# A hybrid attention/RG-LRU step: sums of layer 0 kept in place, first-token products for four blocks, held recurrences, and another grouping of the last columns

## The chip, the cores and the metric

The kernel runs on one core of one Trainium2 chip. The core has five engines, each with a queue of its own that it works off in order: PE (TensorE: matmuls and transposes; its weight loads are shown as PEld), DVE (VectorE), ACT (ScalarE), POOL (GpSimd, which here clears small tiles and issues DMAs) and SP (SyncE, which here only issues DMAs). Matmuls write to PSUM accumulators; DVE and ACT read them out. The metric is the device time of one execution in microseconds (us), as the median of the runs of one kernel.

## The reference, cut to what matters

```python
def reference(x_prompt, x_sample, c, cache_k, cache_v, state_lru, c_ctx, ...):
    y_p, y_s = x_prompt, x_sample            # 128 context tokens, 512 latent tokens, width 2048
    for l in range(2):
        sh, sc, ga = adaln(cond, w_mod[l], b_mod[l])     # once for context, once for latents
        h = rms_norm(y, g_pre[l]) * (1.0 + sc) + sh
        if l == 0: m = attention mixer(h)    # ends in (o * silu(g)) @ w_out_attn
        else:      m = lru_mixer(h)          # below
        y = y + ga * rms_norm(m, g_post[l])

def lru_mixer(h, h0_fwd, h0_bwd, w_in, conv_w, conv_b, w_a, b_a, w_x, b_x, lam, w_out):
    xb, gb = jnp.split(h @ w_in, 2, axis=-1)
    xb = centred_depthwise_conv(xb, conv_w, conv_b)          # width 4
    for d in (forward, backward):
        a, b = rglru_coeffs(xb, w_a[d], b_a[d], w_x[d], b_x[d], lam[d])
        hs[d] = linear_scan(a, b, h0[d], reverse=d)          # h[t] = a[t] * h[t-1] + b[t]
    return ((hs[0] + hs[1]) * silu(gb)) @ w_out, final states

def rglru_coeffs(x, w_a, b_a, w_x, b_x, lam):                # 8 diagonal blocks of 256 columns
    r = sigmoid(block_diag(x, w_a) + b_a); i = sigmoid(block_diag(x, w_x) + b_x)
    a = exp(8 * r * log_sigmoid(lam))
    return a, sqrt(1 - a * a) * i * x
```

## The kernel before, in words

All tokens are handled together: five tiles of 128 tokens, m = 0 to 3 the latents, m = 4 the context (in the transposed form 644 columns, with small gaps). Each fp32 operand is split into a high and a low part ("hi" and "lo" for activations, "wh" and "wl" for weights), and each product is three matmuls. Weights come from memory in pieces of 1 MB into the four buffers of the tile "raw" (load_w, on SP's queue). split_w turns half a piece into wh (ACT, L179) and wl (DVE, L180), of which there are three pairs.

The order of instructions on each engine is set by the framework's planner when the kernel is built: it walks the program in source order as priority, and puts next on an engine what is ready by its own estimate. On the chip each engine keeps that order. A tile of a pool takes one of a fixed number of buffers ("bufs"), and a new tile under the same tag waits until an earlier one has had its last reader.

The second half of the program, in order:

- The output projection of layer 0 (out_proj, gemm_nat) goes over four groups of 512 columns. A group has three accumulators of the tile "pd": tiles (0, 1), (2, 3) and (4). There are four such accumulators of two PSUM banks each (pool "ps2"). Each is read out with the gate into the tile oG (L780) and squared for its norm (L783). The last group is done in two passes, first tiles (0, 1), then (2, 3) and (4) (LAST, L41).
- finish0 (L803), for each tile: load x into a buffer of "raw" (SP), sum x + r * oG into that buffer (DVE, L797), store it as x1_s (POOL, L808), square and sum (ACT, L810), normalise from that buffer into oG (DVE, L812). Then transpose oG (PE, L825), scale and shift, and write hi and lo of those tokens. It is a generator, so that its steps stand between pieces of other products.
- While tiles 2, 3 and 4 go through finish0, PE multiplies the first 256 tokens (tiles 0, 1) with columns of w_in_lru (gemm_T_cols, matmuls of 256 columns): for blocks 0 and 1, both the x half and the gate half. The results wait in two of the four accumulators (p0s).
- Then eight blocks of 256 columns. Blocks 0 and 1 multiply the other 388 columns, x half and gate half; blocks 2 to 7 multiply all tokens (gemm_T, two matmuls of 322 columns each). The x half is copied to "xp" (one buffer), convolved on DVE (conv, L869 to L876, into xc, xh and xl), the gate half becomes gb (ACT tanh, DVE). Then for each half f of the block: four groups of 12 matmuls, each into an accumulator "pd" read out by an ACT sigmoid (L937) into R or I (two buffers each), then the recurrence: tanh, exp and square root on ACT with table loads between them, products and two scans on DVE, and a store to y_s on POOL (L941 to L961).
- The output projection of layer 1 has the same form; finish1 (L985) loads x1_s into "raw" (L990), sums (L995) and stores the outputs (L996). The final states are transposed and stored by final_state, called by late (L999) when four pieces of weights have been used. gate_cols prepares the gates for it during blocks 3 to 6 and the projection.

## Time and profile before

| | us |
|---|---|
| median of 3 runs (lowest to highest) | 1954.33 (1953.74 to 1959.88) |
| the profiled execution, its own time | 1955.32 |
| its span, first to last instruction | 1953.6 |
| PE busy in the span | 1883.5 (96%) |
| DVE busy | 1323.9 (68%) |
| ACT busy | 865.0 (44%) |
| POOL busy | 133.1 (7%) |
| mean granted TensorE clock | 0.991 of 2.4 GHz |

The profiled execution stands for all runs: its time is within 1 us of their median. A row of a timeline has the start, the duration, the engine and line, the operation, the tiles written and read (out<-in), the size, and in brackets how long the engine had been idle and what ended that. Line numbers are those of the kernel before. Matmuls follow each other in a pipeline, so a matmul's shown duration is longer than the distance to the next one; distances or whole stretches give the rate. "PEclk" is the granted clock as a share of 2.4 GHz, so 0.5 is the level of 1.2 GHz.

### The profile page before, as it was taken

What the parts mean: (1) busy time and instruction counts of PE and PEld (TensorE: products, weight loads), DVE (VectorE), ACT (ScalarE), POOL (GpSimd) and SP (SyncE); (2) the same over time, 40 slices, a digit from 0 to 9 for tenths busy, and PEclk for the clock granted to TensorE, in tenths of its full rate; (3) what the DMA queues carried; (4) which work ended last, traced back from release to release, by engine and by line L of the source; (5) the groups of instructions that cost most, each with busy time, mean ns of one, the idle gap of its engine ahead of it and who ended that gap; (6) DMA issues with size and microseconds to landing.
All of it is one profiled execution on the core that took longest, in us unless ns stands there. A gap on an engine that the chain in (4) does not pass through costs nothing.

```text
span 1953.6 us, 26764 instructions
## 1 busy us (share of the span) xinstructions
PE 1883.5 (96%) x10857; PEld 1673.2 (86%) x10857; DVE 1323.9 (68%) x1846; ACT 865.0 (44%) x1255; POOL 133.1 (7%) x212
## 2 busy tenths in 40 slices
PE   4999999999999899999999989899999999999996
PEld 1567887879999899998888889899999999987885
DVE  3237759758375389998857774875685675798645
ACT  4441223222121388881223565666456456742232
POOL 0000000000000001110000000110010010020000
PEclk9999999999999999999999999999999999999998
DMA  9996535536454212225636673323232232546445
GB/s 342 343 318 209 166 109 183 178 123 200 149 178 158 74 38 74 74 97 174 204 130 211 226 263 109 122 77 117 94 102 92 94 100 64 175 140 212 146 149 216
DMA packets 194892, 304.20 MB, mean 156 GB/s; under 512 B 7232, under 2 KB 124608, under 8 KB 191952
## 3 DMA queue, kind: packets, MB, share of 16 engines
q1 hardware_dynamic: 188800, 276.20, 42.6%
q0 software_dynamic: 5968, 26.28, 3.7%
q8 instruction: 85, 1.39, 0.3%
q14 instruction: 39, 0.32, 0.0%
HBM read 273.03 MB, written 29.43 MB: 155 GB/s over the span
## 4 chain that ended last, share of the span: by engine, by line
PE 83%; DVE 6%; ACT 5%; issue 2%; DMA 2%; SPq 1%; POOL 0%; DVEq 0%; ACTq 0%; POOLq 0%
PE pd L184 22%; PE pd L185 22%; PE pd L186 22%; PE pd L215 2%; PE pm L276 2%; PE pd L217 2%; PE pd L218 2%; PE ph L631 1%; PE pg L184 1%; ACT L937 1%; PE pg L186 1%; PE pg L185 1%; PE sp L184 1%; PE sp L186 1%; PE ph L184 1%
## 5 line engine op out<-in xcount | busy, mean ns | idle before, releaser
L179 ACT CAST wh<-raw 128x1024 fp32r<-128x1024 f32 x248 | 258.1, 1048 | 604.8 <-PE pd L186 323.6
L180 DVE TENSOR_TENSOR wl<-raw,wh 128x1024 fp32r<-128x1024 f32 x248 | 301.4, 1221 | 237.5 <-ACT wh L179 236.6
L184 PE MATMUL pd<-wh,hi 128*128 128x512 f32 x1040 | 410.4, 395 | 5.8 <-ACT pd L783 3.3
L185 PE MATMUL pd<-wl,hi 128*128 128x512 f32 x1040 | 409.9, 394 | 0.0
L186 PE MATMUL pd<-wh,lo 128*128 128x512 f32 x1040 | 409.7, 394 | 0.0
L184 PE MATMUL pd<-hi,wh 128*128 128x322 f32 x1280 | 399.2, 312 | 0.0
L186 PE MATMUL pd<-hi,wl 128*128 128x322 f32 x1280 | 397.0, 310 | 1.1 <-DVE wl L180 1.1
L185 PE MATMUL pd<-lo,wh 128*128 128x322 f32 x1280 | 397.5, 311 | 0.0
L186 PEld LDWEIGHTS pd<-hi,wl 128*128 128x128 f32 x1280 | 241.6, 189 | 1.6 <-DVE wl L180 1.6
L185 PEld LDWEIGHTS pd<-lo,wh 128*128 128x128 f32 x1280 | 242.2, 189 | 0.1
L184 PEld LDWEIGHTS pd<-hi,wh 128*128 128x128 f32 x1280 | 241.4, 189 | 0.5 <-ACT wh L179 0.3
L184 PEld LDWEIGHTS pd<-wh,hi 128*128 128x128 f32 x1040 | 195.5, 188 | 52.5 <-ACT pd L783 3.7
L186 PEld LDWEIGHTS pd<-wh,lo 128*128 128x128 f32 x1040 | 195.4, 188 | 45.9
L185 PEld LDWEIGHTS pd<-wl,hi 128*128 128x128 f32 x1040 | 195.4, 188 | 45.4 <-DVE wl L180 0.3
L741 DVE SCALAR_TENSOR_TENSOR ga<-raw,cT,ga 128x512 f32<-128x512 f32 x256 | 175.5, 744 | 15.2 <-DMA ga<-b_mod 12.4
L395 DVE SCALAR_TENSOR_TENSOR ga<-raw,cT,ga 128x1024 f32<-128x1024 f32 x120 | 149.7, 1278 | 28.1 <-DMA raw<-w_mod 27.5
L215 PE MATMUL pd<-hi,wh 128*128 128x256 f32 (+1 forms) x256 | 80.5, 314 | 6.4 <-ACT wh L179 4.7
L184 PE MATMUL pd<-xh,wh 128*128 128x322 f32 x256 | 81.1, 318 | 5.2 <-ACT xh L875 4.4
L185 PE MATMUL pd<-xl,wh 128*128 128x322 f32 x256 | 80.0, 313 | 0.0
L218 PE MATMUL pd<-hi,wl 128*128 128x256 f32 (+1 forms) x256 | 79.9, 312 | 0.0
L217 PE MATMUL pd<-lo,wh 128*128 128x256 f32 (+1 forms) x256 | 79.8, 312 | 0.0
L186 PE MATMUL pd<-xh,wl 128*128 128x322 f32 x256 | 79.8, 312 | 0.0
(233 smaller groups left out, 2807.3 us busy)
## 6 DMA issues: line engine op xcount, KB each, us to landing
raw<-w_mod SPq DMA_DIRECT2D x64, 1024.0 KB, 5.2
raw<-w_in_lru SPq DMA_DIRECT2D x40, 1024.0 KB, 5.3
raw<-w_in_attn SPq DMA_DIRECT2D x36, 1024.0 KB, 6.1
raw<-w_mod SPq DMA_DIRECT2D x64, 512.0 KB, 8.4
raw<-w_out_attn SPq DMA_DIRECT2D x20, 1024.0 KB, 6.0
raw<-w_out_lru SPq DMA_DIRECT2D x20, 1024.0 KB, 5.3
g_s<-qf POOLq DMA_DIRECT2D x16, 322.0 KB, 3.4
raw<-g_s SPq DMA_DIRECT2D x16, 322.0 KB
```

The source lines that it names most:

```text
L179: S.copy(wh, src)
L180: V.tensor_tensor(wl, src, wh.bitcast(F32), op=sub)
L184: PE.matmul(out, ah, bh, start=first, stop=False)
L185: PE.matmul(out, ah, bl, start=False, stop=False)
L186: PE.matmul(out, al, bh, start=False, stop=last)
L215: PE.matmul(outs[f], wh[:, c], hi[:, k, t], start=(k == 0 and first[f]), stop=False, skip_group_check=True)
L217: PE.matmul(outs[f], wh[:, c], lo[:, k, t], start=False, stop=False, skip_group_check=True)
L218: PE.matmul(outs[f], wl[:, c], hi[:, k, t], start=False, stop=(k == KT - 1), skip_group_check=True)
L276: PE.matmul(pm[32 * j:32 * j + 32], c32[:, kb * 4 + j], raw[:, j * 512:j * 512 + 512], start=(kb == 0), stop=(kb == 3))
L395: V.scalar_tensor_tensor(acc[c], w2[:, k2], cT[:, k, c:c + 1], acc[c], op0=mult, op1=add)
L631: PE.transpose(pt[:, c * 128:c * 128 + 128], P[:, b, c * 128:c * 128 + 128], ident)
L741: V.scalar_tensor_tensor(acc[:, c], raw[:, k4 * 512:k4 * 512 + 512], cT[:, kb * 4 + k4, c:c + 1], acc[:, c], op0=mult, op1=add)
```

## The change

1. finish0: the sum goes into oG itself, and the store and the normalisation work on oG. x of tiles 0, 1 and 3 comes into "raw" as before; x of tiles 2 and 4 comes in two halves of 1024 columns into a buffer of the gates ("Gc") and one of the gate accumulation ("ga"), loaded on POOL's queue: tile 2's at the end of the first pass, tile 4's after tile 2's sum. The square's unused output goes to a tile under the tag "v".
2. The first 256 tokens are multiplied with the x halves of blocks 0 to 3 (NB1 = 4) and no gate halves. Blocks 0 to 3 then multiply 388 columns for x, and all tokens for the gate.
3. The recurrence becomes the function recur. For f = 1 of blocks 0, 1 and 2 it is held and called in the next block, behind that block's convolutions.
4. Layer 1's last column group is done as tiles (0, 1) and (4), then (2) and (3) in accumulators of their own, whose squares go to an SBUF tile. finish1 sums in place in halves; x1 of tiles 0, 1 and 4 comes in halves through two buffers on POOL's queue. final_state is called two pieces later.

```diff
-NB1 = 2
-LAST = [[(0, 1)], [(2, 3), (4,)]]
+NB1 = 4
+LAST = [[[(0, 1)], [(2, 3), (4,)]], [[(0, 1), (4,)], [(2,), (3,)]]]
...
+    def x_halves(p):
+        a = p.tile([128, 2, 512], F32, name="Gc", tag="Gc", bufs=2)
+        b = gpool.tile([128, 2, 512], F32, name="ga", tag="ga")
+        return [t.rearrange("p c n -> p (c n)") for t in (a, b)]
...
-            for grp in ([PAIRS] if n < 3 else LAST):
+            for grp in ([PAIRS] if n < 3 else last):
...
-                        S.activation(a[:, j], a[:, j], AF.Square, accum_out=ss[:, m, n:n + 1])
+                        sq = gpool.tile([128, 512], F32, name="gp", tag="gp") if grp is LAST[1][1] else a[:, j]
+                        S.activation(sq, a[:, j], AF.Square, accum_out=ss[:, m, n:n + 1])
...
+    def halves():
+        return [(t, lambda a, b=b: a[:, b * 1024:b * 1024 + 1024]) for b, t in enumerate(x_halves(pd))]
+    def fetch(m, pieces):
+        held_x[m] = pieces
+        for x, cut in pieces:
+            G.dma_start(x, cut(x_rows(m)))
...
-                xt = x1_tile(m, oG, r, j, x_rows(m))
-                G.dma_start(x1_s[m], xt)
+                pieces = held_x.pop(m) if m in held_x else whole(rawp.tile([128, 2048], F32, name="raw", tag="raw"))
+                if m in (0, 1, 3):
+                    SY.dma_start(pieces[0][0], x_rows(m))
+                for x, cut in pieces:
+                    V.scalar_tensor_tensor(cut(oG[:, m]), cut(oG[:, m]), r[:, j:j + 1], x, op0=mult, op1=add)
+                if m == 2:
+                    fetch(4, halves())
+                G.dma_start(x1_s[m], oG[:, m])
                 sx = small.tile([128, 1], F32, name="sx", tag="sx")
-                S.activation(oG[:, m], xt, AF.Square, accum_out=sx)
+                S.activation(pd.tile([128, D], BF16, name="vj", tag="v", bufs=2), oG[:, m], AF.Square, accum_out=sx)
                 r1 = rstd_of(sx, 1, D, "r1")
-                V.tensor_scalar(oG[:, m], xt, r1, None, op0=mult)
+                V.tensor_scalar(oG[:, m], oG[:, m], r1, None, op0=mult)
...
+        if len(grp) == 1:
+            fetch(2, halves())
...
     for blk in range(NB1):
-        p0 = psd()
-        p0s.append(p0)
-        for e in range(2):
-            gemm_T_cols([p0[:, e, 0:256], p0[:, e, 256:512]], w_l, e * D + blk * 256, slice(0, 256),
-                        lambda: next(rest, None), (True, False))
+        if blk % 2 == 0:
+            p0s.append(psd())
+        p0 = p0s[blk // 2][:, blk % 2]
+        gemm_T_cols([p0[:, 0:256], p0[:, 256:512]], w_l, blk * 256, slice(0, 256),
+                    lambda: next(rest, None), (True, False))
...
+    def recur(blk, f, R, I, xc, gb):
...
         if blk < NB1:
-            p0 = p0s[blk]
-            t2 = slice(256, TW)
+            p0 = p0s[blk // 2][:, blk % 2]
             n2 = TW - 256
-            px, pg = psd(), psd()
...
+            px = psd()
+            gemm_T_cols([px[:, 0, :n2], px[:, 1, :n2]], w_l, blk * 256, slice(256, TW), lambda: None, (True, True))
+            src = [[(1, p0[:, f * 256:f * 256 + 256]), (257, px[:, f, :n2])] for f in range(2)]
         else:
             acc = gemm_T(w_l, blk * 256)
+            src = [[(1 + h * TH, acc[f][:, h, :TH]) for h in range(2)] for f in range(2)]
+        for f in range(2):
+            xp = pad()
+            for at, a in src[f]:
+                S.copy(xp[:, at:at + a.shape[1]], a)
+            xcs.append(conv(xp, blk * 2 + f))
+        while held:
+            recur(*held.pop())
+        acc = gemm_T(w_l, D + blk * 256)
...
+            if f and blk < NB1 - 1:
+                held.append((blk, f, R, I, xcs[f][0], gbs[f]))
+            else:
+                recur(blk, f, R, I, xcs[f][0], gbs[f])
...
     def finish1(grp, oG, ss):
...
+                for h in range(2):
+                    c = slice(h * D // 2, (h + 1) * D // 2)
+                    y = oG[:, m, c]
+                    if m in (2, 3):
+                        x = raw[:, c]
+                    else:
+                        x = pf.tile([128, 1024], F32, name="xr", tag="xr", bufs=2)
+                        G.dma_start(x, x1_s[m][:, c])
+                    V.scalar_tensor_tensor(y, y, r[:, j:j + 1], x, op0=mult, op1=add)
+                    (SY if m in (2, 3) else G).dma_start(dst[:, c], y)
+                yield
...
-        if kb == 4:
+        if kb == 6:
             final_state()
```

## Rows read from the trace of the kernel before

**Rows 1.** The page, part 1: busy time of each engine, its share of the span, and its instructions.

```profile
PE 1883.5 (96%) x10857; PEld 1673.2 (86%) x10857; DVE 1323.9 (68%) x1846; ACT 865.0 (44%) x1255; POOL 133.1 (7%) x212
```

**Rows 2.** Whom PE waited for from 1100 us to the end: the line waited for, us in total, times, the longest.

```profile
PE pd L215 <- ACT wh L179: 4.7, 1, 4.7
PE pd L184 <- ACT xh L875: 4.4, 1, 4.4
PE pd L184 <- ACT pd L783: 3.3, 1, 3.3
PE pd L215 <- ACT I L937: 1.7, 1, 1.7
...
PE pd L184 <- ACT R L937: 0.5, 1, 0.5
```

**Rows 3.** Stretches (us from the span's start) and their length; busy us and instructions of PE, PEld, DVE, ACT and POOL; the granted TensorE clock; the DMA engines' share; GB/s. In order: two stretches around the end of layer 0's projection, the first-token stretch, a piece of it with matmuls of 256 columns alone, a product of 388 columns, blocks 0 and 1, the products of block 2, the gates of block 2.

```profile
1102.00:1120.00 18.00, 18.00 (x111) 15.91 (x110) 14.06 (x23) 11.90 (x22) 0.00 (x0) 1.00 0.50 174
1120.00:1140.00 20.00, 14.70 (x114) 14.29 (x113) 16.89 (x36) 10.39 (x13) 1.60 (x3) 0.89 0.91 321
1114.50:1173.20 58.70, 53.40 (x434) 52.94 (x434) 46.77 (x78) 37.42 (x56) 1.73 (x5) 0.94 0.75 250
1162.00:1173.00 11.00, 11.00 (x95) 11.00 (x95) 8.90 (x15) 8.07 (x15) 0.14 (x2) 1.00 0.59 187
1173.20:1190.30 17.10, 17.10 (x99) 17.10 (x98) 5.80 (x5) 4.30 (x5) 0.00 (x0) 1.00 0.44 132
1173.20:1224.30 51.10, 48.89 (x290) 48.15 (x288) 25.77 (x28) 29.84 (x37) 0.27 (x4) 1.00 0.33 103
1224.30:1278.90 54.60, 50.18 (x289) 49.92 (x290) 39.99 (x40) 36.55 (x43) 8.83 (x16) 0.97 0.33 109
1278.90:1336.10 57.20, 57.20 (x387) 57.06 (x386) 44.84 (x45) 26.76 (x29) 8.48 (x16) 1.00 0.38 122
1336.10:1350.60 14.50, 14.44 (x98) 14.18 (x97) 3.94 (x4) 14.20 (x16) 0.00 (x0) 1.00 0.01 1
```

**Rows 4.** The chain of work that ended last, in order of time: start, us, what.

```profile
1111.94 0.23 PE pd L184
...
1127.62 8.57 DMA raw<-w_in_lru
...
1152.83 1.75 PE pd L825 x16
```

**Rows 5.** Timeline of POOL: the issue of tile 3's store of x1.

```profile
1126.76 0.53 POOL L808 DMA_DIRECT2D x_s<-raw  x1 [2.86 <-DVE raw L797]
```

**Rows 6.** Timeline of DVE: the sum of tile 1, the normalisations of tiles 0 and 1, and of tile 3.

```profile
1086.82 2.35 DVE L797 SCALAR_TENSOR_TENSOR raw<-oG,rr,raw 128x2048 f32<-128x2048 f32 x1
...
1094.28 2.48 DVE L812 TENSOR_SCALAR oG<-raw,rr 128x2048 f32<-128x2048 f32 x2
...
1133.13 1.28 DVE L812 TENSOR_SCALAR oG<-raw,rr 128x2048 f32<-128x2048 f32 x1
```

**Rows 7.** The five stores of x1 (L808), from issue to landing.

```profile
DMA to landing us min/median/max: 4.1/5.3/8.2
```

**Rows 8.** Timeline of DVE: in block 0 the second convolution's first step, its last (xl), the recurrence of f = 0 from its first to its last product; in block 1 the first convolution's first step, the second's last; in block 2 the second gate accumulator's readout.

```profile
1197.67 0.61 DVE L869 TENSOR_SCALAR xc<-xp,VB 128x644 f32<-128x644 f32 x1
...
1203.07 0.83 DVE L876 TENSOR_TENSOR xl<-xc,xh 128x644 fp32r<-128x644 f32 x1 [0.46 <-ACT xh L875]
...
1217.68 1.50 DVE L950 TENSOR_TENSOR I<-I,xc 128x1288 f32<-128x1288 f32 x1 [5.08 <-ACT I L937]
...
1236.62 0.82 DVE L960 SCALAR_TENSOR_TENSOR R<-R,gb 128x642 f32<-128x642 f32 x1
...
1245.98 0.61 DVE L869 TENSOR_SCALAR xc<-xp,VB 128x644 f32<-128x644 f32 x1
...
1264.78 0.83 DVE L876 TENSOR_TENSOR xl<-xc,xh 128x644 fp32r<-128x644 f32 x1
...
1338.41 0.82 DVE L914 SCALAR_TENSOR_TENSOR gb<-gb,pd 128x644 f32<-128x644 f32 x1
```

**Rows 9.** The sixteen stores of a recurrence's result (L961), from issue to landing.

```profile
DMA to landing us min/median/max: 2.5/2.7/3.6
```

**Rows 10.** Timeline of ACT in the gates of block 2: a table load, the first sigmoid, then (left out) a tanh, a load, exp and a load, and the second sigmoid.

```profile
1337.86 1.28 ACT L937 ACT_TABLE_LOAD   x1
1339.16 0.81 ACT L937 ACTIVATE R<-pd,VC 128x644 f32<-128x644 f32 x1
...
1344.35 0.80 ACT L937 ACTIVATE I<-pd,VC 128x644 f32<-128x644 f32 x1
```

**Rows 11.** Timeline of PE between the first and the second column group of layer 1's projection.

```profile
1765.23 0.27 PE L966 MATMUL pd<-ident,st 128*32 128x128 f32 x1
1768.76 0.50 PE L184 MATMUL pd<-wh,hi 128*128 128x512 f32 x1 [3.26 <-ACT pd L783]
```

**Rows 12.** Timeline of DVE behind the last matmuls: readout of tile 4, released by the last matmul, the first sum, the last four sums.

```profile
1938.80 0.69 DVE L780 TENSOR_TENSOR oG<-pd,Gc 128x512 f32<-128x512 f32 x1 [0.18 <-PE pd L186]
...
1941.81 1.28 DVE L995 SCALAR_TENSOR_TENSOR raw<-oG,rr,raw 128x1024 f32<-128x1024 f32 x1
...
1944.34 4.87 DVE L995 SCALAR_TENSOR_TENSOR raw<-oG,rr,raw 128x1024 f32<-128x1024 f32 x4
```

**Rows 13.** The stores of the outputs (L996), from issue to landing.

```profile
DMA to landing us min/median/max: 2.7/5.2/10.7
```

More of the change, by code (lines that the diff above doesn't have):

```diff
@@ L755, in drain, with out_proj @@
             pass
-    def out_proj(w, p, gc, Gs, finish, late=None, double=()):
+    def out_proj(w, p, gc, Gs, finish, last, late=None, double=()):
         oG = p.tile([128, 5, D], F32, name="oG")
@@ L792, in post_rstd, with whole @@
         return rstd_of(st[:, :k], k, D, f"ro{k}")
-    def x1_tile(m, oG, r, j, src):
-        raw = rawp.tile([128, 2048], F32, name="raw", tag="raw")
-        SY.dma_start(raw, src)
-        V.scalar_tensor_tensor(raw, oG[:, m], r[:, j:j + 1], raw, op0=mult, op1=add)
-        return raw
     xs = ExitStack()
     pd = pool("pd", 1, stack=xs)
+    held_x = {}
+    def whole(t):
+        return [(t, lambda a: a)]
+    def halves():
[4 more added lines that the diff above has]
+            G.dma_start(x, cut(x_rows(m)))
     def finish0(grp, oG, ss):
@@ L877, in conv @@
         return xc, xh, xl
+    def recur(blk, f, R, I, xc, gb):
+        ft = blk * 2 + f
+        T = pe.tile([128, 2, TW], F32, name="T", tag="T", bufs=1)
+        for d in range(2):
+            S.activation(T[:, d], R[:, d], AF.Tanh, scale=ct[:, d * 16 + ft:d * 16 + ft + 1])
+        for d in range(2):
+            S.activation(R[:, d], R[:, d], AF.Exp, scale=ce[:, d * 16 + ft:d * 16 + ft + 1])
+        V.scalar_tensor_tensor(T, R, 1.0, T, op0=add, op1=mult)
+        V.tensor_scalar(R, T, -1.0, 1.0, op0=mult, op1=add)
+        G.memset(R[:, :, NL:PO], 0.0)
+        V.scalar_tensor_tensor(T, T, -2.0, T, op0=add, op1=mult)
+        S.activation(T, T, AF.Sqrt, scale=-1.0)
+        V.tensor_tensor(I, I, xc.unsqueeze(1).to_broadcast([128, 2, TW]), op=mult)
+        V.tensor_tensor(I, I, T, op=mult)
+        G.memset(I[:, :, NL:PO], 0.0)
+        G.tensor_copy(I[:, 1, NL:NL + 1], VC[:, 96 + 16 + ft:97 + 16 + ft])
+        V.tensor_tensor_scan(T[:, 0, :TE], R[:, 0, :TE], I[:, 0, :TE], VC[:, 96 + ft:97 + ft], op0=mult, op1=add)
+        V.tensor_tensor_scan(T[:, 1, :TE][:, ::-1], R[:, 1, :TE][:, ::-1], I[:, 1, :TE][:, ::-1], 0.0,
+                             op0=mult, op1=add)
+        G.tensor_copy(st[:, 0, ft:ft + 1], T[:, 0, TE - 1:TE])
+        G.tensor_copy(st[:, 1, ft:ft + 1], T[:, 1, PO:PO + 1])
+        V.tensor_tensor(R[:, 0, :TE], T[:, 0, :TE], T[:, 1, :TE], op=add)
+        V.scalar_tensor_tensor(R[:, 0, :TE], R[:, 0, :TE], 0.5, gb[:, :TE], op0=mult, op1=mult)
+        G.dma_start(y_s[ft][:, :TE], R[:, 0, :TE])
     pfs = []
+    held = []
     gc1 = gate_cols(1, pfs, gates[1])
@@ L916, in hybrid_step @@
+        while held:
+            recur(*held.pop())
+        acc = gemm_T(w_l, D + blk * 256)
+        for f in range(2):
+            g = pe.tile([128, TW], F32, name="gb", tag="gb", bufs=3)
+            g2 = g.rearrange("p (h t) -> p h t", h=2)
+            S.activation(g2, acc[f][:, :, :TH], AF.Tanh, scale=0.5)
+            V.scalar_tensor_tensor(g2, g2, 1.0, acc[f][:, :, :TH], op0=add, op1=mult)
+            gbs.append(g)
         raw = rawp.tile([128, 2048], F32, name="raw", tag="raw")
@@ L1001, in late @@
             load_y(KT - 2)
-        if kb == 4:
+        if kb == 6:
             final_state()
-    drain(out_proj(i["w_out_lru"][0], pf, gc1, gates[1], finish1, late))
+    drain(out_proj(i["w_out_lru"][0], pf, gc1, gates[1], finish1, LAST[1], late))
 _INS = ["x_prompt", "x_sample", "c", "cache_k", "cache_v", "state_lru", "c_ctx", "w_mod", "b_mod", "g_pre",
```

63 lines of the change are left out of this document (6 added, 57 removed).

## The prediction

> **What bounds the kernel now.** I read the busy shares first: PE works 96% of the span [rows 1]. So an edit pays only where PE stands still or runs at a lower clock, and the next view is the list of PE's waits from 1100 us on [rows 2]. Four stand out: 4.7 us for a weight split, 4.4 us for a convolution's cast (xh), 3.3 us for a Square in the output projection, 1.7 us for a gate's evacuation. The table of stretches [rows 3] turns waits into losses, as it holds the clock too. The chain of waits and the queues then say who was late [rows 4].
>
> All sums are made against the profiled execution, 1955.3 us (span 1953.6), 1.0 above the median of the runs, 1954.3. I subtract the gain from 1955.3, then 1.0.
>
> **Part A, end of layer 0: sums in place, x in halves.** The stretch 1114.5 to 1173.2 is 58.7 us. Its work is 384 matmuls of 256 columns (95 of them in 11.0 us, 0.116 each: 44.5) and 48 transposes (16 in 1.75: 5.3), so 49.8. Lost: 8.9, of which 4.7 is the wait for the weight split; after it PE ran partly at 1.2 GHz (mean clock 0.94) [rows 2 to 4]. Why: the load of that weight went out at 1127.62 and took 8.6 us. Of the four "raw" buffers three were held by x of tiles 2, 3 and 4, each until its normalisation (L812), which for tile 3 ended at 1134.4 [rows 4, 6]. The change puts the sum into oG, so a raw buffer is free after the sum (L797), and tiles 2 and 4 don't use one at all. In 1102 to 1120 the DMA engines are half idle (0.50), in 1120 to 1140 at 0.91 [rows 3]: two more weights can come early. That wait should go whole.
>
> What is late next is a new wait. The store of x1 now reads oG, and the normalisation overwrites oG, so on DVE it must wait until the store has landed, 4.1 to 8.2 us after its issue [rows 7]. Behind it on DVE stand weight splits (wl); PE waits for them, and for the transposes. For tile 1 the sum ends near 89.2 (in us after 1000), so a store of 5.3 to 8.2 us lands at 94.9 to 97.8, against a normalisation of tiles 0 and 1 that starts at 94.3 and reaches tile 1 at about 95.5 [rows 6]. That is 0 to 2.5 us late; I take 1.5. For tiles 2 and 3: POOL must first issue the two halves of x for tile 4, two issues of 0.5 us; the store of tile 3 goes out at about 127 and lands at 131 to 135.5, where the second normalisation began at 133.1 [rows 5, 6]. Late by 0 to 2.5, for a PE that asks at 131.4. With the DMA engines at 0.91 I take 2.5, up to 5 if both stores are slow. Splitting the sums of tiles 2 and 4 in two costs about 0.2 us each, under PE's work. So 4.0 of the 8.9 come back as waits; if all stores land early, none. **A gains 4.9** (1 to 8.9).
>
> **Part B, blocks 0 to 3.** Matmuls are the same: four first-token products, four of 388 columns, four full gate products. Work of a new block: 17.1 + 28.6 (half of 57.2) + 14.5 = 60.2; four are 240.8. Blocks 0 and 1 now take 51.1 and 54.6, block 2 takes 57.2 + 14.5 = 71.7, block 3 has the same steps: 249.1 [rows 3]. Lost now: 8.3. The large wait in it (4.4, with the clock at 0.97) is block 1, where conv and the recurrence of block 0 shared DVE: a pair of convolutions ends 13.6 us after its product when alone (1190.3 to 1203.9), but began 4.7 and ended 24 us after it here (1241.3, 1246.0, 1265.6) [rows 3, 8]. With 28.6 us of gate product between x and the gates, instead of 17, and f = 1's recurrence put behind, that wait goes.
>
> Against it stands PSUM. The pool has four accumulators ("pd", two banks each). Both first-token tiles now hold x halves, the first until block 1's copies, the second until block 3's. Block 0 has two left, blocks 1 and 2 three, later ones four. What that costs is read from block 0 of before, where the first gates also had no more than three: waits of 0.5 and 1.7, 2.2 together [rows 2]. With four, a whole gate stage runs in 14.5 without one [rows 3]. With two no row exists, so I bound it from the gates of block 2 [rows 8, 10]. After the gate product PE does the first group of 12 matmuls (1.8); the second waits for the second accumulator, read out at 3.1 us (1336.1 to 1339.2): 1.3 lost. ACT then does a table load, the first sigmoid, a tanh, and exp between two more loads; the second sigmoid ends 9.0 us in, so the fourth group, ready at 6.9, waits 2.1. The same load, exp and load meet the sixth group (2.3) and the square root the eighth or the next block (2.8). Sum 8.5. The other end is 2.2. No row says where between; I take the middle, 5.4. In blocks 1 and 2 I take 2.2 each. The second gate accumulator must also wait for x's copies, since there is one "xp" buffer: 7 us after the product, when the second convolution begins (1190.3 to 1197.7, [rows 8]), against 3.6 (or 7.2 in another order) of work on the first; 0.5 in block 0, 0.8 in block 1. In all 11.1 against 8.3: **B loses 2.8** (gain 4 to loss 9).
>
> Here a rule of the Trainium skill (ScalarE: Activation LUTs, What ACT_TABLE_LOAD costs) speaks against the change: a switch of tables is stated as 2.66 us, a load of 1.28 and a drain of 1.38. The rows show 1.28 and the next sigmoid 0.02 us behind it [rows 10], so the trace bears out the load and not the drain; by the page the four loads in front of the late sigmoids would cost 5.5 us more (4 x 1.38), and the sum would be a gain of 1.9 instead of 7.4.
>
> **Part C, final_state two steps later.** The transpose of the states at 1765.23 took the fourth accumulator just as the next column group wanted it; PE stood until a Square freed another, 3.3 us [rows 2, 11]. With it free, PE starts at once with 12 matmuls of 512 columns (0.23 each, [rows 4]: 2.8), and needs the next accumulator at 1768.2, which came free at about 1768.7: 0.5 stays. At the new place the transpose stands inside a group, with the fourth accumulator unused. **C gains 2.8** (2.3 to 3.3).
>
> **Part D, the tail.** Same matmuls, tiles regrouped. Now PE's last matmul releases DVE at 1938.8; sums start at 1941.81 and are six of 1.2 us, the last ending at 1949.2, and the stores follow [rows 12]. After: tile 2 and tile 3 alone, four sums. Tile 2's accumulator is done six matmuls (1.4 us) before PE's end, as that of tiles 2 and 3 is now; its chain of small steps still takes about 1.7 behind the Square: sums start near 2.7 after PE's end (now 3.0) and end near 7.7 (now 10.4). So 2.7 earlier. Against it: the x halves of tiles 0, 1, 4 come through two buffers on POOL's queue, each refill behind a sum and a store, 3 MB in and 3 MB out in the 22 us of the last group, while SP loads x for tiles 2 and 3. Stores of this output took up to 10.7 us [rows 13]; if DVE waits for such a half, the tail's readout stands behind it. I take 0.2 for that, so **D gains 2.5** (-3 to 3.3).
>
> The rest has one answer, none: Square's junk goes to tiles not in use then; the x halves hold the tile "ga" until tile 4's sum, so layer 1's first gate buffer is cleared later, but it is used only from block 3 on; POOL, busy 7%, has room for the moved issues [rows 1].
>
> **Sum:** 4.9 - 2.8 + 2.8 + 2.5 = 7.4. 1955.3 - 7.4 = 1947.9; less 1.0: **1947**, 0.37% faster. The ends of the parts don't fall together; 2 to 14 us of gain is the forecast's own range, 1940 to 1953.
>
> **Rivals.**
> 1. *Cover holds everywhere.* Stores land before the normalisations, and two accumulators cost no more than three did: A 8.9, B 8.3 - (3 x 2.2 + 0.5) = 1.2, C 2.8, D 2.8. That is 15.7: 1938.6. For it: the second normalisation stood in a DVE queue that was late for other reasons [rows 6]. Against it: the DMA share of 0.91 [rows 3]. Chance 0.20.
> 2. *The waits only move.* Stores late (A 1), two accumulators at the upper end (B: 8.5 + 1.3 + 4.4 = 14.2 against 8.3, so -5.9), C 2.8, D 0: -2.1, that is 1956.4. For it: block 0 waited with three accumulators already. The change then does not remove idle time but puts it into block 0. Chance 0.16. (The Trainium skill, Perfetto Trace Analysis, Identifying Performance Opportunities, reads a gap that repeats on the engine to be kept busy as a possible lack of PSUM; by that, blocks 0 to 2 would show it, and the rows of block 0 agree in kind.)
> 3. *Slower: the held recurrences are late.* R and I have two buffers. The gates for f = 1 in blocks 1, 2 and 3 need the ones that the held recurrence of the block before gives back with its store. PE asks 28.6 + 9.1 = 37.7 us after the 388-column product. Held work: convolutions 13.6, a recurrence 19.8 (1217.7 to 1237.4), the store 2.7: 36.1 [rows 8, 9]. Under two microseconds are spare. If the two mix on DVE as in 1246 to 1266, the convolutions end at 24, the store lands at 46.5, and after two more groups into free accumulators (3.6) PE stands some 5 us in three blocks, 15 to 18 us: 1965. It decides where a store lands later than 37.7. Against it: DVE's recurrence for f = 1 can begin in its idle time before the convolutions. Chance 0.09.
>
> **How the numbers follow.** Forecast 0.55, rivals 0.20, 0.16, 0.09. A measurement of this kernel tells about 0.3% (5.9 us) from no change, so faster means below 1948.5. Of the forecast's 0.55 about 0.32 lie there, 0.22 above, 0.01 slower; rival 1 is faster, rival 2 within, rival 3 slower: faster 0.52, same 0.38, slower 0.10. The range must leave out no more than 2 in 10: 1936 to 1958 takes in most of rivals 1 and 2 and leaves out rival 3 and their outer edges, some 0.18.
>
> **What would show it.** A: no 4.7 us wait for wh in the first-token stretch, but waits of the transposes for DVE, and DVE idle for DMA before L812's successor. B: PE gaps of 1 to 3 us in the gates of block 0, smaller ones in 1 and 2, none for xh. C: no wait for a Square near the second column group. D: four sums behind the last matmul. If block 0's gates run in 14.5 the term of 5.4 was wrong; if block 1 to 3 wait for R, rival 3.

## The result, and the profile after

| | us |
|---|---|
| before, median of 6 runs (lowest to highest) | 1954.36 (1951.8 to 1959.88) |
| after, median of 6 runs | 1966.38 (1963.39 to 1966.68) |
| ratio, 95% interval | 1.0052 (1.0035 to 1.0068) |
| the profiled execution of after; its span | 1963.39; 1961.4 |

The change makes the kernel 0.5% slower; 0.4% faster had been predicted, with 1958 as the upper end. The profiled span is 7.8 us longer than that of before. The other 4 of the 12 us between the medians are not in these two profiles: the profiled run of before was 1.0 above its median, that of after is 3.0 below and the fastest of its six.

PE is as full as before [rows 1]; whom it waits for is another list (page, part 1; then the waits of PE from 1060 us on, with us in total, times, the longest):

```profile
PE 1886.7 (96%) x10857; PEld 1674.0 (85%) x10857; DVE 1322.9 (67%) x1854; ACT 869.5 (44%) x1267; POOL 148.1 (8%) x226
```

```profile
PE pd L184 <- ACT I L979: 6.3, 5, 2.0
PE pd L847 <- DVE oG L834: 4.7, 3, 2.0
PE pd L215 <- ACT R L979: 3.1, 1, 3.1
PE pd L184 <- ACT pd L790: 2.8, 1, 2.8
PE pd L184 <- ACT R L979: 2.3, 3, 1.9
PE pd L184 <- ACT xp L947: 0.8, 1, 0.8
...
```

The two large waits of before, for a weight (4.7) and for xh (4.4), are gone [rows 2]. In their place stand sigmoids (L979: 6.3, 3.1 and 2.3), normalisations (L834: 4.7) and a Square (L790: 2.8).

Stretches of the changed kernel, columns as in [rows 3]: the first-token stretch, blocks 0, 1, 2 and 3, and the time behind PE's last matmul.

```profile
1117.25:1172.60 55.35, 52.77 (x433) 52.09 (x432) 46.53 (x80) 36.60 (x55) 3.77 (x8) 0.97 0.74 246
1172.60:1243.50 70.90, 62.54 (x386) 61.24 (x384) 30.97 (x30) 35.97 (x41) 1.43 (x7) 0.98 0.24 75
1243.50:1308.00 64.50, 62.22 (x385) 61.36 (x385) 37.14 (x36) 35.41 (x41) 8.40 (x13) 0.97 0.28 91
1308.00:1369.80 61.80, 60.29 (x385) 59.71 (x384) 47.59 (x49) 41.62 (x47) 12.17 (x16) 1.00 0.36 113
1369.80:1430.00 60.20, 60.15 (x386) 59.88 (x385) 46.08 (x48) 39.76 (x44) 10.30 (x16) 1.00 0.37 117
...
1946.60:1961.40 14.80, 0.00 (x0) 0.00 (x0) 10.17 (x22) 1.67 (x6) 1.08 (x2) 0.67 0.66 262
```

The point of these rows is that the same work (some 385 matmuls in each block) takes 70.9, 64.5, 61.8 and 60.2. Block 3 is what a block costs when nothing waits.

From the starts of PE's instructions the program is cut into stages, from PE's last matmul before the first transposes of layer 0's end on (us):

| kernel | end of layer 0, to block 0 | blocks 0 to 3 | blocks 4 to 7 | layer 1's projection | behind PE's end |
|---|---|---|---|---|---|
| before | 77.6 | 249.1 | 286.4 | 230.1 | 14.8 |
| after | 77.3 | 257.4 | 286.7 | 229.8 | 14.8 |

So blocks 0 to 3 lose 8.3; the end of layer 0 and the projection gain 0.3 each, and the tail nothing. A stage varies by 2 to 5 us between the profiles of kernels that share it (last table below), so 0.3 is no gain. Four readings say why.

**Block 0.** Timeline of ACT in its gates:

```profile
1221.49 0.80 ACT L979 ACTIVATE R<-pd,VC 128x644 f32<-128x644 f32 x1
1222.32 0.84 ACT L908 ACTIVATE T<-R,ct 128x644 f32<-128x644 f32 x1
1223.17 1.28 ACT L910 ACT_TABLE_LOAD   x1
1224.47 0.83 ACT L910 ACTIVATE R<-R,ce 128x644 f32<-128x644 f32 x1
1225.32 1.28 ACT L979 ACT_TABLE_LOAD   x1
1226.62 0.80 ACT L979 ACTIVATE I<-pd,VC 128x644 f32<-128x644 f32 x1
...
1236.56 1.28 ACT L915 ACT_TABLE_LOAD   x1
1237.85 1.28 ACT L915 ACTIVATE T<-T 128x1288 f32<-128x1288 f32 x1
...
1241.38 1.28 ACT L979 ACT_TABLE_LOAD   x1
1242.68 0.80 ACT L979 ACTIVATE R<-pd,VC 128x644 f32<-128x644 f32 x1
```

From the first sigmoid to the second it is 5.1 us, with tanh, exp and two loads between; between the sixth and the seventh the square root. With two accumulators PE stands for each (the rows of PE's timeline that waited in this stage, and the first matmul of block 1):

```profile
1222.34 0.42 PE L184 MATMUL pd<-xh,wh 128*128 128x322 f32 x1 [1.94 <-ACT R L979]
...
1227.47 0.42 PE L184 MATMUL pd<-xh,wh 128*128 128x322 f32 x1 [1.31 <-ACT I L979]
```

With those at 1233.3 (2.0) and 1243.5 (3.1) it is 8.4, and PE's clock falls under full speed: 0.98 in block 0, 0.97 in block 1.

**End of layer 0.** The stores of x1 (L830) land 6.8/9.4/11.1 us after their issue (minimum, median, maximum) against 4.1/5.3/8.2 [rows 7]. Tile 0's, issued at 1085.8, takes 9.4 (5.2 before). Just behind it SP loads two more weights, for which the sum in place has left buffers free; before, the first of these came only at 1093.43, when that store had landed (timelines of SP, the changed kernel and the kernel before):

```profile
1086.65 2.63 SPq L170 DMA_DIRECT2D raw<-w_in_lru  x2
```

```profile
1093.43 0.37 SPq L170 DMA_DIRECT2D raw<-w_in_lru  x1
```

The normalisation (L834) waits for four of five of them, from the view of that line (its idle time, then who waited for it; us, times):

```profile
  DMA x_s<-oG: 6.1, 4
...
  PE pd L847: 4.7, 3
```

**Second column group of layer 1.** PE now does run on with 12 matmuls there, up to 1776.3, and then waits for a Square:

```profile
1779.08 0.49 PE L184 MATMUL pd<-wh,hi 128*128 128x512 f32 x1 [2.79 <-ACT pd L790]
```

Behind this wait the clock stayed at full speed in this run, as it did behind the 3.3 of the kernel before (1.00 there too); experiments 1 and 13 show that it need not (stretch, columns as above):

```profile
1779.00:1785.00 6.00, 5.92 (x26) 4.83 (x27) 2.23 (x3) 3.83 (x9) 0.95 (x1) 1.00 0.69 260
```

Behind that wait are POOL's two early x loads, SP's load of y_s, ACT's cast of what it brings, and DVE's queue up to the readout (timelines of POOL, SP, ACT, DVE):

```profile
1755.06 1.19 POOL L1024 DMA_DIRECT2D xr<-x_s  x2
```

```profile
1758.00 0.34 SPq L999 DMA_DIRECT2D raw<-y_s  x1
```

```profile
1765.97 0.73 ACT L1000 CAST hi<-raw 128x642 fp32r<-128x642 f32 x1 [12.22 <-DMA raw<-y_s]
```

```profile
1767.48 3.40 DVE L741 SCALAR_TENSOR_TENSOR ga<-raw,cT,ga 128x512 f32<-128x512 f32 x5
...
1776.37 2.94 DVE L786 TENSOR_TENSOR oG<-pd,Gc 128x1024 f32<-128x1024 f32 x3
```

The y_s load took 8.0 us (1758.0 to 1766.0), with the DMA engines at 0.97; in the kernel before it took 5.0, with the DMA engines at 0.93 (timelines of SP and ACT there):

```profile
1749.73 0.34 SPq L975 DMA_DIRECT2D raw<-y_s  x1
```

```profile
1754.73 0.73 ACT L976 CAST hi<-raw 128x642 fp32r<-128x642 f32 x1 [9.09 <-DMA raw<-y_s]
```

DVE's multiplications for the gate queue up behind it, and the readouts (L786) behind these.

**The tail.** Timeline of DVE: tile 4's first sum waits for its x on POOL's queue, and the readouts of tiles 2 and 3, whose matmuls end at about 1945.2 and 1946.6, stand behind it:

```profile
1947.28 1.28 DVE L1025 SCALAR_TENSOR_TENSOR oG<-oG,rr,xr 128x1024 f32<-128x1024 f32 x1 [4.80 <-DMA xr<-x_s]
1948.48 1.28 DVE L786 TENSOR_TENSOR oG<-pd,Gc 128x512 f32<-128x512 f32 x2
...
1952.34 2.48 DVE L1025 SCALAR_TENSOR_TENSOR oG<-oG,rr,raw 128x1024 f32<-128x1024 f32 x2
```

### The profile page after: what moved, and what is told of

Same layout as the page of the kernel before. It is cut to its first block, busy times and chain, and to the rows that moved or that the text cites. A ratio compares the mean times of both kernels' runs of the same rounds, so it can differ in the third digit from the quotient of the medians.

```text
span 1961.4 us, 26793 instructions
## 1 busy us (share of the span) xinstructions
PE 1886.7 (96%) x10857; PEld 1674.0 (85%) x10857; DVE 1322.9 (67%) x1854; ACT 869.5 (44%) x1267; POOL 148.1 (8%) x226
```

## The experiments

Unless said otherwise each is the changed kernel with one edit. Ratios are to the kernel before, run on the same chip.

**1. Sigmoids first.** A data dependency keeps the recurrence of f = 0 behind the eighth sigmoid.

```diff
-            if f and blk < NB1 - 1:
+            if blk < NB1 - 1:
                 held.append((blk, f, R, I, xcs[f][0], gbs[f]))
+                if f:
+                    recur(*held.pop(0), I[:, 1, 0:1])
...
-    def recur(blk, f, R, I, xc, gb):
+    def recur(blk, f, R, I, xc, gb, behind=None):
...
+        for d in range(2 if behind is not None else 0):
+            V.tensor_copy(T[:, d, 0:1], behind)
```

> The changed kernel with one edit: in blocks 0 to 2 the recurrence of f = 0 (tanh, exp, square root on ACT) starts only behind the eighth sigmoid of its block (its first tanh depends on the last sigmoid's output through a one-column copy on DVE). Nothing is left out. Theory 1 (with two accumulators free, each table load and exp between two sigmoids becomes a wait of PE): the waits in the gates of block 0, 9.0 us in the changed kernel with the one in front of the next 388-column product, fall to 1 to 3; those of blocks 1 and 2 (1.8 each) go; block 4 starts 8 to 10 us earlier and the time is 1956 to 1959. Theory 2 (two accumulators are too few whatever ACT does between the sigmoids, because matmuls and readout alternate): waits of 5 us or more stay in block 0, and the time stays above 1962. Theory 3 (the recurrence that starts later is late for the buffers R, I or T of the next block): new waits for R in blocks 1 to 3, time as before the edit or slower.

1951.3 us, ratio 0.9988 (0.9978 to 0.9997). Theory 1, with a few us more than it gave. (Its 9.0 counts the four waits of 8.4 from start to start.) ACT now waits for PE between sigmoids, not PE for ACT (ACT's timeline in block 0):

```profile
1223.88 0.80 ACT L981 ACTIVATE R<-pd,VC 128x644 f32<-128x644 f32 x1
1228.10 0.80 ACT L981 ACTIVATE I<-pd,VC 128x644 f32<-128x644 f32 x1 [3.42 <-PE pd L186]
1230.13 0.80 ACT L981 ACTIVATE R<-pd,VC 128x644 f32<-128x644 f32 x1 [1.23 <-PE pd L186]
```

Blocks 0 to 3 take 245.8, block 0 63.9. One wait of 1.9 is left in it, for the first sigmoid, which stands behind a load after the tanh of gb. The profiled run, 1959.1, is the slowest of its ten: at the second column group PE stood 3.5 us, then ran at half clock, and the projection took 235.1 (the stretch behind the wait):

```profile
1772.00:1778.00 6.00, 5.93 (x14) 4.67 (x15) 2.28 (x3) 2.75 (x8) 0.95 (x1) 0.50 0.69 262
```

**2. A third accumulator.**

```diff
+    p01 = pe.tile([128, 512], F32, name="p01", tag="p01")
+    S.copy(p01, p0s[0][:, 1])
...
-            p0 = p0s[blk // 2][:, blk % 2]
+            p0 = p01 if blk == 1 else p0s[blk // 2][:, blk % 2]
```

> The changed kernel with one edit: ACT copies block 1's first-token half from the first accumulator into SBUF ahead of block 0 (one copy of 512 columns), so the first accumulator is free once block 0's x is copied: block 0's gates have three accumulators instead of two, block 1's gates and its gate product three. ACT's order of table loads and sigmoids stays. Theory 1 (accumulators held by the first-token halves): block 0's waits fall from 9.0 us to about the 2.2 that the kernel before had with three, and the 1.0 us wait in block 1's gate product for the copy of xp goes: 6 to 8 us, 1958 to 1960. Theory 2 (the table loads alone set the pace of the gates, the number of accumulators is not what is short): 9.0 stays within 2 us, 1964 to 1967.

1953.7 us, ratio 0.9996 (0.9986 to 1.0005). Theory 1, and with more than it gave: blocks 0 to 3 take 246.1, block 0 62.2 instead of 70.9, at full clock:

```profile
1174.50:1236.70 62.20, 60.63 (x387) 59.79 (x385) 25.04 (x25) 29.84 (x36) 0.27 (x4) 1.00 0.27 85
```

Above the 60.2 of work, block 0 now loses 2.0 with the loads between sigmoids but three accumulators, 3.7 in experiment 1 with two but without the loads, and 10.7 with both.

**3. x of tile 0 later, x of tile 4 by SP.**

```diff
-                if m in (2, 3):
+                if m >= 2:
                     raw = rawp.tile([128, 2048], F32, name="raw", tag="raw")
...
+                        if m == 0:
+                            G.tensor_copy(x[:, 0:1], oG[:, 0, 0:1])
                         G.dma_start(x, x1_s[m][:, c])
```

> The changed kernel with two edits in its last stage: the two x halves of tile 0 are loaded only after tile 0's first readout of layer 1's projection (POOL copies one column of oG into the tile first), and x of tile 4 comes as one load on SP's queue into a raw buffer. Theory 1 for the wait of 3.0 us at the second column group (the early x loads lie beside the load of y_s, which took 7.9 us instead of 5.0, and DVE's work behind it holds up the readout): the y_s load takes about 5, the readout starts 2 to 3 us earlier relative to PE, and the wait falls to 0.5. Theory 2 (the gate's multiplications on DVE are late for another reason, as the weight loads): the wait stays at 2.5 to 3. For the tail, theory 1 (DVE stands 4.8 us for tile 4's half on POOL's queue): that wait goes, the last sum ends 2.5 to 3.5 us earlier relative to PE's end (now 11.2 behind it). Both together 5 to 6: 1960 to 1961; if both theories fail, 1965 to 1967.

1965.5 us, ratio 1.0056 (1.0041 to 1.0071). At the second column group theory 1: the y_s load takes 4.9, PE has no wait at all from 1700 us on, and the projection takes 227.0 instead of 229.8. In the tail the wait only moved, to tile 1's second half, ahead of tile 3's readout:

```profile
1950.00 1.28 DVE L1027 SCALAR_TENSOR_TENSOR oG<-oG,rr,xr 128x1024 f32<-128x1024 f32 x1 [4.42 <-DMA xr<-x_s]
```

Behind PE's end stand 16.9 us now, so the time gains nothing.

**4. Sums apart.** For tiles 0, 1 and 3 (sep) the sum goes to the raw buffer (xt), which is stored, squared and normalised from.

```diff
-                    V.scalar_tensor_tensor(cut(oG[:, m]), cut(oG[:, m]), r[:, j:j + 1], x, op0=mult, op1=add)
+                    V.scalar_tensor_tensor(x if sep else cut(oG[:, m]), cut(oG[:, m]), r[:, j:j + 1], x,
+                                           op0=mult, op1=add)
...
-                V.tensor_scalar(oG[:, m], oG[:, m], r1, None, op0=mult)
+                V.tensor_scalar(oG[:, m], xt, r1, None, op0=mult)
```

> The changed kernel with one edit at the end of layer 0: for tiles 0, 1 and 3 the sum goes into the raw buffer that holds x (as in the kernel before), is stored from there, and the normalisation reads it from there into oG; tiles 2 and 4 stay in place. Theory 1 (the normalisation waits for the store, as it overwrites what the store reads): the waits in front of the transposes of tiles 0 and 1 (1.3 and 1.7 us) go, the one for tiles 2 and 3 (2.2) falls to what tile 2's store leaves of it; against that three raw buffers are held longer than in the changed kernel and a part of the wait for a weight may come back, 0 to 2. Gain 3 to 5 before block 0: 1962 to 1963. Theory 2 (the transposes wait for the sums or Squares, not for the store): the waits stay, 1966.

1959.6 us, ratio 1.0026 (1.0015 to 1.0037). Theory 1: PE waits for no normalisation, the stage takes 73.3, and no wait for a weight came back. Tile 0's store, now from the buffer of x, lands after 5.0 us. What is left there:

```profile
PE pd L850 <- ACT v L857: 2.1, 1, 2.1
```

**5. Nothing held.**

```diff
-            if f and blk < NB1 - 1:
+            if False:
```

> The changed kernel with one edit: no recurrence is held back; f = 1 of blocks 0 to 2 is issued in its own block, as in the kernel before. Theory 1 (the held order is what removed the 4.4 us wait for xh): waits for xh of 2 to 5 us come back in block 1, perhaps in 2 and 3, and the time is 3 us or more above the changed kernel. Theory 2 (the gate product of 28.6 us between x and the gates is cover enough: in the kernel before, the mixed convolutions ended 24 us behind their product): no wait for xh, and blocks 0 to 3 take the changed kernel's 257.5 within 1.5 us.

1966.8 us, ratio 1.0054 (1.0033 to 1.0075). Theory 2: no wait for xh; blocks 0 to 3 take 258.7. That is 1.3 more than in the profile of the changed kernel, but the other kernels with these blocks unedited and held took 257.0 (4) and 258.8 to 259.1 (3, 6, 9 and 13). So holding back gained nothing that shows, and this stage varies by 2 us between profiles, with that of the changed kernel near the lower end.

**6. All x by SP.**

```diff
-                if m in (2, 3):
-                    raw = rawp.tile([128, 2048], F32, name="raw", tag="raw")
-                    SY.dma_start(raw, x1_s[m])
+                raw = rawp.tile([128, 2048], F32, name="raw", tag="raw")
+                SY.dma_start(raw, x1_s[m])
```

> The changed kernel with one edit in its last stage: x of all five tiles comes whole into raw buffers on SP's queue, as in the kernel before; the sums stay in halves and in place, the grouping of tiles stays. Theory 1 (both losses come from x on POOL's queue): the wait at the second column group falls from 3.0 to 0.5 or less, DVE no longer stands 4.8 us for a half, and PE's end to the last sum's end falls from 11.2 to 7.5 to 8.5: in all a gain of 5 to 6, 1960 to 1961. Theory 2 (raw buffers that hold x are missing for weights): PE waits for a weight split in the last group, 2 us or more, and the gain is 3 or less.

1962.6 us, ratio 1.0035 (1.0022 to 1.0047). Both theories have a part. The second column group waits 0.4 and 11.8 us stand behind PE's end; but PE waits for the last weights, and runs at a mean clock of 0.83 there (waits in the last 60 us, and the stretch):

```profile
PE pd L184 <- ACT wh L179: 1.8, 1, 1.8
PE pd L185 <- DVE wl L180: 0.5, 1, 0.5
```

```profile
1935.30:1945.60 10.30, 7.97 (x26) 5.49 (x24) 3.05 (x3) 2.61 (x4) 0.00 (x0) 0.83 0.97 401
```

**7 and 8. All together.** 7 has edits 1, 2, 4 and 6; 8 is 7 with all sums in the buffers of x.

> The changed kernel with all edits together: in blocks 0 to 2 sigmoids ahead of the recurrence, block 1's first-token half copied to SBUF, sums of tiles 0, 1 and 3 apart at the end of layer 0, x of all tiles on SP's queue in the last stage. Theory 1 (the losses are apart from each other and add): from 1963.4 (profiled) go 11.5 in blocks 0 to 3 as the first of these edits showed, 1 to 3 more with the third accumulator, 5.5 at the end of layer 0, 5 to 6 in the last stage: 1938 to 1941, 0.7 to 0.8% faster than the kernel before. Theory 2 (a stage that starts earlier meets loads that come no earlier, so that a part is given back as waits for weights): 1944 to 1950.

> As the kernel with all edits, but at the end of layer 0 every sum goes into the buffers that hold x (for tiles 2 and 4 into the halves), is stored from there in as many pieces, and is normalised from there into oG; x of tile 4 is fetched only after tile 2's normalisation. Theory 1 (the wait of about 2.2 us before the transposes that was left with tiles 2 and 4 in place is the wait for tile 2's or 4's store): it goes, 1 to 2.5 us faster than with tiles 2 and 4 in place. Theory 2 (tile 4's x, now fetched some 6 us later, is late for tile 4's transposes): another wait of 1 to 4 us ahead of these takes its place, same time or slower.

7: 1941.1 us, ratio 0.9927 (0.9909 to 0.9945): theory 1 at its edge. Blocks 0 to 3 take 241.0, the work and nothing else; block 0 takes 60.6. 8: 1946.1, ratio 0.9948 (0.9929 to 0.9967): theory 2, the second half of tile 4's x comes too late, and DVE waits 5.5 us for it; the end of layer 0 takes 77.0 instead of 73.1. Another 1.7 are lost in the projection, where PE waits longer for weights.

**9. Another tail.** x of tiles 0 and 1 whole through one POOL buffer, the first one late; the others by SP.

```diff
+                if m >= 2:
+                    raw = rawp.tile([128, 2048], F32, name="raw", tag="raw")
+                    SY.dma_start(raw, x1_s[m])
+                else:
+                    raw = pf.tile([128, 2048], F32, name="xr", tag="xr")
+                    if m == 0:
+                        G.tensor_copy(raw[:, 0:1], oG[:, 0, 0:1])
+                    G.dma_start(raw, x1_s[m])
```

> The changed kernel with one edit in its last stage: x of tiles 0 and 1 comes whole through one buffer on POOL's queue, that of tile 0 only after tile 0's first readout of layer 1's projection (POOL copies one column of oG into the buffer first), that of tile 1 behind tile 0's sums; x of tiles 2, 3 and 4 through raw buffers on SP's queue. Theory 1 (what was lost is the early x load at the second column group and DVE's stand for a half in the last one; with five raw buffers it was PE's wait for the last weights): wait at the second column group under 0.6, no wait of PE in the last group over 0.6, from PE's end to the end of the span 11 to 12 instead of 14.8: a gain of 5 to 6, 1959 to 1961. Theory 2 (in the last group some transfer is always late, as 3 MB come and go beside the weights): one of the two waits stays or another comes, gain 3 or less.

1961.4 us, ratio 1.0031 (1.0015 to 1.0047). Between the theories: no wait at the second column group and none of PE in the last one, but DVE stands 4.3 us for tile 1's x, and 13.3 us remain behind PE's end.

**10 and 11. The best of each.** 7 with the tail of 9; in 10 tile 4's sum in the halves of its x, in 11 in oG.

> The kernel with all edits together, with two of them changed: the last stage is that of the kernel of this call with x of tiles 0 and 1 through one buffer, and at the end of layer 0 tile 4's sum too goes into the halves that hold its x, with x of tile 4 fetched early as in the changed kernel; tile 2 alone stays in place. Theory 1 (the 2.1 us wait for the first transposes of tile 4 is its store, and the 2.6 us with the clock loss behind it in the last group the raw buffers that hold x): 1.5 to 2.5 less at the end of layer 0, 4 to 5 less in the last stage, against 1941.1: 1934 to 1937. Theory 2 (tile 4's transposes wait for its sums): 1 less at most there, and 1937 to 1939.

> As the kernel before it, with tile 4's sum in place in oG again, so that its normalisation waits for its store. Theory 1: the wait of 2.1 ahead of the transposes of tile 4 is here and not there; 1.5 to 2.5 slower. Theory 2: no difference over 0.5 in the first-token stretch.

10: 1939.1 us, ratio 0.9921 (0.9907 to 0.9935), the fastest with 11: 1939.1, ratio 0.9918 (0.9902 to 0.9935). Theory 1 fails for tile 4: the stage takes 73.6 and 73.2. The wait that is left is not for a store but for ACT's readout of a transposed tile:

```profile
PE pd L855 <- ACT v L862: 2.4, 1, 2.4
```

In 11 the second column group waits 2.2, in 10 0.3, though no x load is early in either; in both the readouts start at the same time (1755.1 and 1754.8), and PE comes 1.6 earlier in 11. That points to DVE's queue, which sets this moment; it wasn't tried by itself.

**12. Part C alone, on the kernel before** (kb 4 to 6 in late, nothing else).

> The kernel before with part C alone: final_state two steps later. Theory 1 (as predicted: the transpose took the accumulator; DVE's readout is early enough when no x load lies beside the load of y_s): PE goes on with 12 matmuls (2.8) at the second column group and waits 0.3 to 1 for the next accumulator instead of 3.3. Theory 2 (DVE's multiplications hold the readout back by themselves): the wait stays at 2.5 to 3 behind the 12 matmuls.

One run, 1950.3 us; eleven of the kernel before took 1952.0 to 1959.2. Theory 1: from the second column group on PE has no wait, and the projection takes 227.0 instead of 230.1.

**13. No x for tile 4.**

```diff
+                    elif m == 4:
+                        x = y
```

> The changed kernel, whose output for tile 4 leaves out the residual: no x is loaded for tile 4, its two sums take oG itself in x's place (same instructions on DVE, 1 MB less of transfers in the last group). All else as changed. Theory 1 (the tail's missing gain is DVE's wait for tile 4's x, behind which the readouts of tiles 2 and 3 stand): from PE's end to the end of the span 14.8 falls to 11 to 12, the 2.5 to 3 of the prediction; the wait at the second column group stays at 3. Theory 2 (the tail is set by its own small steps and stores, not by that x): 14.8 stays within 0.5.

1963.6 us, ratio 1.0043 (1.0028 to 1.0057). Theory 1: the readouts start when their matmuls end, and 11.5 us stand behind PE's end instead of 14.8 (DVE's timeline, and the stretch):

```profile
1948.33 0.69 DVE L786 TENSOR_TENSOR oG<-pd,Gc 128x512 f32<-128x512 f32 x1 [2.45 <-PE pd L186]
1949.73 0.69 DVE L786 TENSOR_TENSOR oG<-pd,Gc 128x512 f32<-128x512 f32 x1 [0.71 <-PE pd L186]
```

```profile
1949.70:1961.20 11.50, 0.00 (x0) 0.00 (x0) 7.15 (x19) 1.03 (x5) 0.00 (x0) 0.63 0.45 182
```

The profiled span hardly shows these 3.3 (1961.2 against 1961.4), as the projection takes 233.0 instead of 229.8: behind the wait at the second column group, 3.2 here, the clock fell.

```profile
1779.40:1785.40 6.00, 5.89 (x14) 4.63 (x15) 2.14 (x3) 2.80 (x8) 0.95 (x1) 0.50 0.70 264
```

**14. Number 10 with tile 1's sums behind the readouts** (their factor goes through one DVE operation that reads tile 3's readout).

> The kernel of 1939.1 (all edits, x of tiles 0 and 1 through one buffer) with tile 1's two sums behind the readouts of tiles 2 and 3 (their factor goes through one column of DVE that reads tile 3's readout). Theory 1 (readouts that stand behind a late x on DVE cost the tail): DVE's readouts start within 1 us of the matmuls that release them, and from PE's end to the end of the span 13.3 falls to 11.5 to 12.5. Theory 2 (the sums only change places, as all six must end before the last store): 13.3 stays within 0.5.

1940.0 us, ratio 0.9923 (0.9908 to 0.9938). Theory 2: the readouts are in time, but six sums follow them, and 13.9 us stand behind PE's end.

The stages of those runs, as above (us):

| kernel | end of layer 0 | blocks 0 to 3 | projection | behind PE's end |
|---|---|---|---|---|
| 1 sigmoids first | 79.5 | 245.8 | 235.1 | 14.9 |
| 2 third accumulator | 80.4 | 246.1 | 231.6 | 14.8 |
| 3 x late | 78.8 | 258.8 | 227.0 | 16.9 |
| 4 sums apart | 73.3 | 257.0 | 231.5 | 14.5 |
| 5 nothing held | 76.5 | 258.7 | 231.4 | 15.2 |
| 6 all x by SP | 77.0 | 258.8 | 231.9 | 11.8 |
| 7 all | 73.1 | 241.0 | 232.5 | 11.8 |
| 8 all sums in x | 77.0 | 241.0 | 234.2 | 11.8 |
| 9 another tail | 78.5 | 258.9 | 227.1 | 13.3 |
| 10 best | 73.6 | 241.0 | 227.3 | 13.3 |
| 11 tile 4 in place | 73.2 | 241.0 | 229.3 | 13.3 |
| 12 part C alone | 76.7 | 249.1 | 227.0 | 14.8 |
| 13 no x for tile 4 | 76.5 | 259.1 | 233.0 | 11.5 |
| 14 tile 1 behind | 72.8 | 241.3 | 227.8 | 13.9 |

## Why the prediction was wrong

The places were right: each of the four parts did what was said and met the wait that was named for it (part C another one). Every counter-term was too small, and rival 2, "the waits only move", is nearest to what happened, with more lost in B than its sum had.

**A, predicted 4.9, found 0.3.** The wait for the weight went whole, as said, and the gain without store waits is shown: 4.3 with the sums apart (77.6 to 73.3). It is clear of the spread: the stage takes 72.8 to 73.6 in experiments 4, 7, 10, 11 and 14, and 76.5 to 80.4 in the eight kernels with all sums in place. The step that failed is "4.0 of the 8.9 come back". The store was taken at 4.1 to 8.2 us from the kernel before; in the changed kernel it lands after 6.8 to 11.1. DVE waited for four stores, tile 0's among them (1.2 us), which the prediction took as landed. PE lost 4.7 to it, and part of the clock (0.97). The 1.5 for tile 1 was also taken out of the wrong stretch: the 8.9 belong to the stretch that starts with the first-token products, in which 5.5 are still lost (55.35 less 49.8), while the waits for the stores of tiles 0 and 1 lie ahead of it and cost 2.9 more there (21.9 against 19.0).

Why the first store is slower can be read from the runs. In all eight kernels with the sums in place SP issues three weight loads from 0.3 us before to 3.1 behind tile 0's store, and it lands after 9.0 to 9.5; in all eight others it is one load until 7.4 behind, and the store lands after 5.0 to 5.2. So the freed buffers, which are this part's gain, are also what lets loads run beside the stores. The store's source changes with them, and no run separates the two.

**B, predicted a loss of 2.8, found 8.3.** The mis-sized term is the two accumulators: "no row says where between; I take the middle, 5.4" out of 2.2 to 8.5. The walk through ACT's queue that gave 8.5 was right: 8.4 of waits were measured, 1.9, 1.3, 2.0 and 3.1 where it had 1.3, 2.1, 2.3 and 2.8. But the sum also left out the clock that such waits cost. All in all blocks 0 and 1 took 10.7 and 4.3 above the work of 60.2, where 5.9 and 3.0 had been taken. Experiments 1 and 2 show the cause from both sides. The gain term held, but for one of its two reasons: the gate product of 28.6 us covers the convolutions by itself, and holding the recurrences adds nothing that shows (experiment 5). Rival 3 did not occur.

The Trainium skill's figure for a switch of tables (ScalarE: Activation LUTs, What ACT_TABLE_LOAD costs), with a drain of 1.38 above the load, is not borne out: in block 0 a load takes 1.28, starts 0.01 to 0.02 behind the instruction ahead of it, and the next one starts 0.01 to 0.02 later.

**C, predicted 2.8, found 0.3.** The mechanism was right: alone it gains 3.1 (experiment 12), and in the changed kernel PE ran the 12 matmuls. What failed is the step that let DVE's readout be where it was, so that 0.5 of waiting would stay; 2.8 stayed. Part D's first two x loads wait for nothing, so POOL issues them at 1755.1, 175 us ahead of their use and beside the load of y_s, on which DVE's queue hangs. Experiment 3 takes them away and the wait goes. It holds over all runs: in the six kernels with these two loads (the changed one, 1, 2, 4, 5, 13) the y_s load takes 8.0 to 8.6 and PE waits 2.8 to 3.5 for the Square; in those with the change and without the loads it takes 4.7 to 6.4, and PE waits 1.1 at most, but for the 2.2 of experiment 11. The prediction had looked for these loads only in the last group. The 0.3 is the lucky side: in the other five with the loads the 6 us behind the wait ran at a mean clock of 0.50 to 0.74, and the projection takes 231.4 to 235.1, more than the 230.1 of before. The Trainium skill (Trainium Kernel Development and Optimization, Key Constraints) says that transfers issued from SP, ACT and POOL run on the same DMA engines and interleave; the 8.0 us instead of 5.0 agree.

**D, predicted 2.5, found 0.** The regrouping is worth 3.3 behind PE's end (14.8 to 11.5) when no x is late (experiment 13). The step that failed is "I take 0.2 for that": DVE stood 4.8 us for tile 4's half. No place that was tried for the x loads was free: SP's raw buffers then lack for weights, and POOL's one buffer makes tile 1's x late, with the DMA engines at 0.91 from 1910 us to PE's end at 1925 (experiment 10). Here the prediction's range (-3 to 3.3) held; only the value was too friendly.

So A, C and D together came out 9.6 below their sum, and B 5.5; the other 4 are the distances of the two profiled runs from their medians. The 3.0 of the changed kernel may lie in any of three stages in which kernels that share them with it took longer: up to 3.1 at the end of layer 0 (experiment 2), 1.7 in blocks 0 to 3 (experiment 13) and 5.3 in the projection, with the clock behind its wait (experiment 1). Which it was in its other five runs stays open, as these have no trace. So does why the later stores of x1 are slower too (median of the five 9.4 here, 7.4 in experiment 4, 5.3 before).

## What to carry to other kernels

When a change takes accumulators away, walk through the reading engine's queue with the number that is left, and where the walk gives a wait, take it whole, with the clock that is lost behind it; a middle between it and a stage that had more buffers is no estimate. A transfer with nothing to wait for is issued as soon as its queue gets to it: look for it where it starts, not where it is used, and bound it to something late if its stretch is tight. In-place results that are stored and then overwritten put the store's landing on the path. And a stage read from one profile can be off by some us (the projection with the same edits took 229.8 to 235.1): look how far it varies between kernels that share it before a small difference is called a gain.

## What was not expected of the hardware

Two costs that are small alone are large together: above 60.2 of work block 0 loses 0.4 us with three accumulators and no table loads between the sigmoids (experiment 7), 2.0 with three and loads, 3.7 with two and no loads, and 10.7 with two and loads. A 1 MB store to memory took 5.3, 7.4 or 9.4 us as the median in three kernels that differ in where its source lies and what else is in flight. And a stand of PE cost no clock in one run and half of it in another: behind 3.3 us at the second column group it stayed at 1.00 in the kernel before, behind 3.2 it fell to 0.50 in experiment 13.
